# One transformer layer on one core: sixteen modulation products moved to the input projection, the retention's norm by a square root on ScalarE, and elementwise work reassigned between output and up projection

## Chip, cores and metric

One core of one Trainium2 chip runs the whole layer. The metric is device time in microseconds. The kernel before has a median of 2920.0 us over 3 runs (2919.52 to 2924.84).

## What is computed

A layer for one sequence of T = 1024 tokens with D = 1024 channels, all in fp32: a norm and a shift and scale from a condition vector, one input projection into nine parts, two mixers (retention over decayed states, and differential attention), a gated merge, and a feed-forward block with a depthwise convolution. Cut to what matters here:

```python
cond = silu(c)
mod = cond @ w_mod + b_mod
sh1, sc1, g1, sh2, sc2, g2 = split(mod, 6)
p = (x * (1 + sc1) + sh1) @ w_in
qr, kr, vr, gr, qd, kd, vd, gate_r, gate_d = project_heads(p)
y = retention(qr, kr, vr) + reversed_retention(qr, kr, vr)
y = (y - mean(y)) * rsqrt(var(y) + 1e-5)
y_ret = (silu(gr) * y) @ w_ret_out
y_dif = readout(diff_attention(qd, kd, vd)) @ w_diff_out
y_mix = (sigmoid(gate_r) * y_ret + sigmoid(gate_d) * y_dif) @ w_o
x = layer_norm(alpha * x + g1 * y_mix)
u, gate = split((x * (1 + sc2) + sh2) @ w_up)
y_ff = (gelu(dwconv(u)) * gate) @ w_down
x = layer_norm(alpha * x + g2 * y_ff)
```

## The kernel before

Every product is made in three parts. `split` (lines 83 to 86) writes the high half of an operand by a cast on ACT (line 85) and the low half by a subtraction on DVE, or on POOL where it is told so (line 71); `mm3` (line 257) then issues three matmuls, high by high, high by low and low by high. Weights come through a ring of buffers: `w_cols` and `load_split` issue the load on SP, then split it on ACT and DVE.

The stages follow one another on TensorE. After the norm of x come the projections of the attention's queries and keys, of its values (`proj_N`, tiles `pxn`), of the retention's queries and keys, and of its values (`proj_N` again). A call of `proj_N` is one group of 512 columns: four 512 KB loads of `w_in` ahead of it, and five steps of 256 tokens (four and the context). Then comes the attention, then the retention.

In the **retention** (4 heads, 4 chunks of 256 tokens, two directions) `turn` transposes keys, `update` makes a state S by matmuls (`pS`) and a DVE step and splits it (`sh` on ACT; `sl`, one half of it on DVE and one on POOL), `scores` makes the masked scores (`pa`, `am`), `outputs` makes y (`py`), copies it to `z` on ACT, takes mean and variance on DVE, and normalises; `send` transposes z, multiplies by the gate `g` and stores it. The norm's 1/sqrt is `ln_rstd`: thirteen DVE instructions on [128, 2] values (an integer estimate and three Newton steps) and one more for the shift `nb`; the normalisation is a POOL tensor_scalar on `z`.

In the **output projection** (tiles `py`, 12 groups in three passes: attention, and two halves of the retention's output) each group's product is multiplied on DVE by a sigmoid gate (`ga`) and added on POOL. Between the groups of passes two and three, two steps of the generator `mods` are taken. A step (`mod_one`, line 293) makes 256 columns of the modulation: two 512 KB loads of `w_mod` (`mr`, two buffers), one DVE tensor_scalar (line 297) and seven DVE multiply-adds (`md`, line 77), and a small matmul that sums over partitions; 8 of the 16 end in a column table (`pc`, `mcol`), the 8 of g1 and g2 in rows broadcast to all partitions (`pb`, `bmr`, `mrow1`, `mrow2`):

```python
        fill = mods()
...
                if n:
                    next(fill, None)
                    next(fill, None)
```

Then comes w_o (tiles `pxo`, eight blocks of 128 tokens). After a block `norm1` normalises it, and during the next `turned` transposes it (`pth`), scales and shifts it (`m`; half the operations on ACT, half on DVE) and splits it. The up projection forms seven products per tile of columns from sums and differences of quarters of the weights and of the tokens; `weights_first` makes the first of the former during block 7, `sum_split` the splits of the latter (`s6l`, `s7l`, `s3l`) after it, while block 7 itself is normalised and turned. Then the up projection runs 22 tiles, and the down projection with the last norm ends the kernel.

The program is written in this order, and a scheduler then sets the order of the instructions of each engine, in the retention above all; each engine and SP's queue then keep that order.

Of the kernel before, what the change touches and what calls it, by code (L numbers as in the profile page):

```python
# [8 lines left out]
F32 = mybir.dt.float32  # L9
# [55 lines left out]
def build(nc, tc, A, out, upto=99, dbg=None):  # L65
# [44 lines left out]
    d_tab = dram("d_tab", [HR, P, 896])  # L110

# [69 lines left out]

    def ln_rstd(pool, var, n, name):
        w = pool.tile([P, n], F32, name=name + "_w", tag=name + "_w")
        ts(w, var, EPS, 1.0, ALU.add, ALU.mult)
        return rsqrt(w, n, pool, name + "_rs")
# [107 lines left out]
    def mod_one(pool, raw, seg, row):  # L293
# [144 lines left out]
    with ExitStack() as ph:  # L438
# [72 lines left out]

        def proj_N(c0, dst, d0, want_ctx, func):

            ws = w_cols(w_in, c0, 512)
            for b in range(0, 10 if want_ctx else 8, 2):
# [8 lines left out]
                ST.dma_start(out=dst[b * P:b * P + 256, d0:d0 + 512].rearrange("(a p) n -> p a n", p=P), in_=st)  # L524

# [293 lines left out]
    with ExitStack() as ph:  # L819
# [34 lines left out]
        def update(h, c, d):  # L854
# [7 lines left out]
            for a in range(2):  # L862
# [8 lines left out]
                split(sh[:, a, :], sl[:, a, :], new[:, a, :], G if a else V)  # L871
# [34 lines left out]
        def outputs(h, c):  # L906
# [134 lines left out]
    with ExitStack() as ph:  # L1041
        wp = ph.enter_context(tc.tile_pool(name="p4", bufs=1))
        def mods():
            for c in range(16, 48, 2):
                o = {2: (mrow1, c - 16), 5: (mrow2, c - 40)}.get(c // 8)
                row = None if o is None else o[0][:, o[1] * P:o[1] * P + 256]
                mod_one(wp, lambda i: wp.tile([P, 1024], F32, name="mr", tag="mr", bufs=2), c, row)
                yield

# [11 lines left out]
        fill = mods()  # L1061
# [8 lines left out]
        for at, (n, g) in enumerate(groups):  # L1070
# [46 lines left out]
        for _ in fill:  # L1117
            pass
# [169 lines left out]
    for b in range(8):  # L1288
# [230 lines left out]
```

## Time and profile before

| | |
|---|---|
| median of 3 runs | 2920.0 us |
| profiled execution | 2915.08 us, its span 2913.3 us |
| busy: PE, DVE, ACT, POOL | 2798.5, 1714.0, 1058.0, 770.5 us |
| mean granted clock of TensorE | 0.984 of full speed |
| retention, 1478 to 1800 us | PE busy 291.44 us of 322 |
| output projection, 1800 to 2100 us | PE busy 276.56 us of 300 |
| w_o, 2100 to 2202 us | PE busy 101.53 us of 102 |
| passage to the up projection, 2202 to 2262 us | PE busy 37.95 us of 60 |

The stages are read by windows, since their limits differ: PE's share is 96% over all, but it leaves 30.6, 23.4 and 22.1 us idle in three of these windows. Busy time of PE includes the time in which it ran at a lower clock, so a window's mean clock belongs beside it.

### The profile page before, as it was taken

How to read it: one execution, taken by the hardware profiler on the slowest of the kernel's cores; microseconds unless marked ns; L12 is line 12 of the kernel's file. 1: busy time of each engine (PE TensorE's matmuls, PEld its weight loads, DVE VectorE, ACT ScalarE, POOL GpSimd, SP SyncE). 2: the span in 40 equal slices, each digit the busy share in tenths (PEclk: the TensorE clock that was granted, in tenths of full speed). 3: DMA queues.
4: the chain of work that ended last, by engine and by line, in shares of the span. 5: the costliest groups of instructions: out<-in, count | busy, mean ns of one | idle time of the engine just before them, and what ended most of it. 6: DMA issues, size and time to landing. Idle time of an engine off the chain costs nothing.

```text
span 2913.3 us, 34764 instructions
## 1 busy us (share of the span) xinstructions
PE 2798.5 (96%) x13610; PEld 2334.0 (80%) x13610; DVE 1714.0 (59%) x2442; ACT 1058.0 (36%) x1465; POOL 770.5 (26%) x503
## 2 busy tenths in 40 slices
PE   7999999999999999999988998999896999999997
PEld 5888888888888888888876777877685888887886
DVE  4852133201267777667779997367866555547666
ACT  4321210111245555444554554223334444444221
POOL 3321022100000000000045553034433333336744
PEclk9999999999999999999999999999998999999999
DMA  8544322422233233323143425475421322224321
GB/s 249 180 149 143 103 87 94 152 80 73 75 101 107 83 103 104 103 98 89 53 139 112 129 95 202 137 253 192 162 80 44 109 87 80 87 75 171 138 94 58
DMA packets 262309, 340.17 MB, mean 117 GB/s; under 512 B 15559, under 2 KB 193152, under 8 KB 262144
## 3 DMA queue, kind: packets, MB, share of 16 engines
q1 hardware_dynamic: 223840, 258.50, 27.8%
q10 hardware_dynamic: 38304, 79.45, 7.7%
q8 instruction: 107, 1.75, 0.2%
q14 instruction: 58, 0.48, 0.1%
HBM read 242.72 MB, written 95.16 MB: 116 GB/s over the span
## 4 chain that ended last, share of the span: by engine, by line
PE 77%; DVE 12%; DMA 5%; issue 2%; POOL 2%; ACT 1%; SPq 0%; DVEq 0%; POOLq 0%; ACTq 0%
PE pg L257 18%; PE px L257 12%; PE pxn L257 11%; PE pu L257 8%; PE pyd L257 6%; PE sp L707 5%; PE py L257 4%; PE po L257 4%; PE tp L731 2%; PE pxo L257 2%; DMA mr<-in_w_mod 2%; PE pcx L257 2%; DVE md L77 1%; DVE ql L71 1%; DVE S L77 1%
## 5 line engine op out<-in xcount | busy, mean ns | idle before, releaser
L71 DVE TENSOR_TENSOR wl<-wraw,wh 128x1024 fp32r<-128x1024 f32 (+1 forms) x234 | 311.5, 1339 | 488.8 <-ACT wh L85 485.9
L85 ACT CAST wh<-wraw 128x1024 fp32r<-128x1024 f32 (+1 forms) x234 | 219.5, 947 | 494.3 <-PE pu L257 135.7
L710 DVE TENSOR_SCALAR_CACHE_REDUCE e<-sp 128x1280 f32<-128x1280 f32 x128 | 190.6, 1489 | 106.6 <-PE sp L707 105.8
L71 POOL TENSOR_TENSOR rd<-ident,wh 128x512 fp32r<-128x512 f32 x16 | 17.7, 1107 | 852.0 <-ACT wh L85 817.1
L82 ACT ACTIVATE e<-e,m 128x1280 f32<-128x1280 f32 x128 | 175.0, 1367 | 186.0 <-DVE e L710 186.0
L71 POOL TENSOR_TENSOR wraw<-wraw 128x512 f32<-128x512 f32 x86 | 152.4, 1772 | 264.2 <-DVE wl L71 259.7
L257 PE MATMUL pg<-xH,wl 128*128 128x512 f32 x496 | 194.7, 393 | 0.0
L257 PE MATMUL pg<-xH,wh 128*128 128x512 f32 x496 | 194.7, 393 | 0.0
L257 PE MATMUL pg<-xL,wh 128*128 128x512 f32 x496 | 194.4, 392 | 0.0
L71 POOL TENSOR_TENSOR rp<-rp,rp 128x1024 f32<-128x1024 f32 x32 | 88.8, 2799 | 374.3 <-DVE rp L71 374.3
L707 PE MATMUL sp<-ks,qd 128*128 128x512 f32 (+1 forms) x768 | 174.1, 362 | 1.1 <-DVE e L710 1.1
L257 PE MATMUL py<-opH,wh 128*128 128x512 f32 x384 | 153.7, 406 | 20.1 <-DVE ga L71 15.5
L257 PE MATMUL px<-xL,wh 128*128 128x512 f32 x512 | 158.1, 390 | 0.0
L257 PE MATMUL px<-xH,wl 128*128 128x512 f32 x512 | 157.6, 389 | 0.0
L257 PE MATMUL px<-xH,wh 128*128 128x512 f32 x512 | 156.9, 391 | 0.0
L257 PE MATMUL py<-opL,wh 128*128 128x512 f32 x384 | 153.7, 400 | 1.4 <-DVE opL L71 1.3
L257 PE MATMUL py<-opH,wl 128*128 128x512 f32 x384 | 153.2, 399 | 0.0
L257 PE MATMUL pxn<-wh,xH 128*128 128x512 f32 x384 | 149.4, 389 | 0.0
L257 PE MATMUL pxn<-wl,xH 128*128 128x512 f32 x384 | 149.4, 389 | 0.0
L257 PE MATMUL pxn<-wh,xL 128*128 128x512 f32 x384 | 149.4, 389 | 0.0
L707 PEld LDWEIGHTS sp<-ks,qd 128*128 128x128 f32 x768 | 129.6, 188 | 23.4 <-DVE e L710 2.7
L257 PEld LDWEIGHTS px<-xL,wh 128*128 128x128 f32 x512 | 95.8, 188 | 21.2 <-issue 0.8
(362 smaller groups left out, 7105.6 us busy)
## 6 DMA issues: line engine op xcount, KB each, us to landing
wraw<-in_w_in SPq DMA_DIRECT2D x88, 512.0 KB, 4.0
wraw<-in_w_up SPq DMA_DIRECT2D x44, 512.0 KB, 3.7
qd<-d_qd SPq DMA_DIRECT2D x128, 128.0 KB, 3.0
mr<-in_w_mod SPq DMA_DIRECT2D x32, 512.0 KB, 5.0
ga<-d_ga SPq DMA_DIRECT2D x24, 512.0 KB, 5.4
d_u<-u SPq DMA_DIRECT2D x22, 512.0 KB, 2.6
fl<-d_u SPq DMA_DIRECT2D x22, 512.0 KB, 5.1
wraw<-in_w_down SPq DMA_DIRECT2D x22, 512.0 KB, 5.8
```

Source lines behind the costliest of these rows:

```text
L71: eng.tensor_tensor(out=o, in0=a, in1=b, op=op)
L77: V.scalar_tensor_tensor(out=o, in0=a, scalar=s, in1=b, op0=op0, op1=op1)
L82: return S.activation(out=o, in_=a, func=func, bias=bias, scale=scale, accum_out=accum)
L85: S.copy(out=h, in_=x)
L257: PE.matmul(ps[:, c:e], w, m[:, c:e], start=start and i == 0, stop=stop and i == 2, skip_group_check=more)
L707: st["pe"] = PE.matmul(sp[:, a:b], w, r["k"][c][:, a:b], start=part == 0, stop=part == 1).ins
L710: V.tensor_scalar(out=e, in0=sp[:, :TK], scalar1=-0.125, scalar2=None, op0=ALU.mult, op1=ALU.min, accum_out=m)
L731: PE.transpose(tp[:, k, :], a[:, k * P:(k + 1) * P], ident)
```

## The change

- `mods` is taken in the input projection, one step at b = 0, 4 and 8 of each `proj_N`. The rows of g1 and g2 are computed on one partition, stored by ACT's DMA queue into a new DRAM array `d_row`, and loaded broadcast into `mrow1` and `mrow2` in group 3 of the output projection.
- The retention's norm uses `rstd_shift` (lines 168 to 180): a square root on ACT, a reciprocal on DVE, seven [128, 1 or 2] instructions on POOL. `z` is normalised by two ACT activations. Both halves of `sl` go to POOL.
- `turned` scales and shifts on ACT alone. `weights_first` becomes `first_raws` (loads and POOL differences, in block 4) and `first_splits` (block 7). The large parts of `s7l` and `s3l` go from POOL to DVE.
- In the up projection product 3 comes before product 4 from the second tile on, and the copy and the addition of products 5 and 7 change places.

```diff
@@ retention
-                split(sh[:, a, :], sl[:, a, :], new[:, a, :], G if a else V)
+                split(sh[:, a, :], sl[:, a, :], new[:, a, :], G)
...
-            rs = ln_rstd(misc, mv[:, :, 1], 2, "lnr")
-            nb = misc.tile([P, 2], F32, name="nb", tag="nb")
-            stt(nb, mv[:, :, 0], -1.0, rs, ALU.mult, ALU.mult)
+            rstd_shift(misc, mv[:, :, 0], mv[:, :, 1], 2, "lnr")
             for b in range(2):
-                ts(zs[b], zs[b], rs[:, b:b + 1], nb[:, b:b + 1], ALU.mult, ALU.add, G)
+                act(zs[b], zs[b], AF.Identity, bias=mv[:, b, 0:1], scale=mv[:, b, 1:2])
@@ mod_one
-            bmr = pool.tile([P, 256], F32, name="bmr", tag="bmr")
-            SP.dma_start(out=bmr, in_=A["b_mod"][:, seg * P:seg * P + 256].broadcast_to([P, 256]))
-            pb = small_ps("pb")[:, 0:256]
-            PE.matmul(pb, onesr.bitcast(F32), md, start=True, stop=True)
-            tt(row, pb, bmr, ALU.add)
+            bmr = pool.tile([1, 256], F32, name="bmr", tag="bmr")
+            SP.dma_start(out=bmr, in_=A["b_mod"][:, seg * P:seg * P + 256])
+            pb = small_ps("pb")[0:1, 0:256]
+            PE.matmul(pb, ones, md, start=True, stop=True)
+            tt(bmr, pb, bmr, ALU.add)
+            ST.dma_start(out=row, in_=bmr)
@@ proj_N
+                if b % 4 == 0:
+                    next(fill, None)
@@ output projection
-                if n:
-                    next(fill, None)
-                    next(fill, None)
+                    for t, r in ((mrow1, 0), (mrow2, 1)):
+                        SP.dma_start(out=t, in_=d_row[r:r + 1, :].broadcast_to([P, D]))
@@ turned
-                if q:
-                    ts(y[:, k, cut], pt[:, j, :], hs[:, 0, k:k + 1], hs[:, 1, k:k + 1], ALU.mult, ALU.add)
-                else:
-                    act(y[:, k, cut], pt[:, j, :], AF.Identity, bias=hs[:, 1, k:k + 1], scale=hs[:, 0, k:k + 1])
+                act(y[:, k, cut], pt[:, j, :], AF.Identity, bias=hs[:, 1, k:k + 1], scale=hs[:, 0, k:k + 1])
@@ w_o
             if n == 5:
+                if b == 4:
+                    first_raws()
                 if b == 7:
-                    weights_first(misc_tile("t2", 1)[:, 0:512])
+                    first_splits()
@@ passage
-    sum_split("7", slice(0, 384), G)
-    sum_split("7", slice(384, 512))
-    sum_split("3", slice(0, 384), G)
-    sum_split("3", slice(384, 512))
+    for n, c in (("6", slice(384, 512)), ("7", slice(0, 384)), ("7", slice(384, 512)), ("3", slice(0, 512))):
+        sum_split(n, c)
@@ up projection
             product(chain, f, 7, False)
-            S.copy(out=g[:, c_hi], in_=chain)
-            tt(g[:, c_hi], g[:, c_hi], p5, ALU.add)
+            tt(g[:, c_hi], g[:, c_hi], chain, ALU.add)
...
+            product(p5, f, 3, False)
+            tt(g[:, c_lo], g[:, c_lo], p5, ALU.add)
             product(chain, f, 4, False)
             S.copy(out=raw[:, c_hi], in_=chain)
-            product(p5, f, 3, False)
-            tt(g[:, c_lo], g[:, c_lo], p5, ALU.add)
```

Three places show what moves. First, DVE in the third pass of the output projection, before (`wl` is the low half of a weight, `ga` the gating):

```order
L77 SCALAR_TENSOR_TENSOR md_16473<-mr_16471,condT_77,md_16473 128x256
L71 TENSOR_TENSOR ga_16339<-py3_16342,ga_16339 128x512
L71 TENSOR_TENSOR wl_16498<-wraw_16494,wh_16497 128x1024
L77 SCALAR_TENSOR_TENSOR md_16473<-mr_16471,condT_77,md_16473 128x256 x3
L71 TENSOR_TENSOR ga_16343<-py3_16346,ga_16343 128x512
L71 TENSOR_TENSOR mrow2_14709<-pb_16466,bmr_16464 128x256
L297 TENSOR_SCALAR md_16627<-mr_16623,condT_77 128x256
L71 TENSOR_TENSOR wraw_16671<-wraw_16671,mrow1_14713 128x1024
L77 SCALAR_TENSOR_TENSOR md_16627<-mr_16623,condT_77,md_16627 128x256 x3
L77 SCALAR_TENSOR_TENSOR md_16627<-mr_16625,condT_77,md_16627 128x256 x3
L71 TENSOR_TENSOR ga_16339<-py3_16342,ga_16339 128x512
L77 SCALAR_TENSOR_TENSOR md_16627<-mr_16625,condT_77,md_16627 128x256
```

and the same place after the change:

```order
L71 TENSOR_TENSOR wl_16266<-wraw_16263,wh_16265 128x1024
L71 TENSOR_TENSOR ga_16141<-py3_16144,ga_16141 128x512
L71 TENSOR_TENSOR ga_16275<-py3_16278,ga_16275 128x512
L71 TENSOR_TENSOR wl_16272<-wraw_16269,wh_16271 128x1024
L71 TENSOR_TENSOR ga_16279<-py3_16282,ga_16279 128x512
L71 TENSOR_TENSOR wraw_16535<-wraw_16535,mrow1_14858 128x1024
L71 TENSOR_TENSOR ga_16275<-py3_16278,ga_16275 128x512
L71 TENSOR_TENSOR wl_16527<-wraw_16523,wh_16526 128x1024
L71 TENSOR_TENSOR ga_16279<-py3_16282,ga_16279 128x512
L71 TENSOR_TENSOR wl_16539<-wraw_16535,wh_16538 128x1024
```

The `md` chains that stood between one gating and the next are gone from this queue.

Second, SP's queue at the passage from the attention's values to the retention's queries and keys, before (`wraw` is a load of weights):

```order
L219 DMA wraw_2401<-in_w_in 128x2x512
L447 DMA sin_2675<-in_k_rope_ret 128x1024
L447 DMA cos_2673<-in_k_rope_ret 128x1024
L219 DMA wraw_2407<-in_w_in 128x2x512
L219 DMA wraw_2677<-in_w_in 128x4x256
L219 DMA wraw_2683<-in_w_in 128x4x256
L219 DMA wraw_2799<-in_w_in 128x4x256
L219 DMA wraw_2805<-in_w_in 128x4x256
```

and after:

```order
L215 DMA wraw_2465<-in_w_in 128x2x512
L215 DMA wraw_2788<-in_w_in 128x4x256
L303 DMA bmr_2318<-in_b_mod 1x256
L263 DMA mr_2523<-in_w_mod 128x4x256
L263 DMA mr_2525<-in_w_mod 128x4x256
L303 DMA bmr_2441<-in_b_mod 1x256
L263 DMA mr_2646<-in_w_mod 128x4x256
L263 DMA mr_2648<-in_w_mod 128x4x256
L215 DMA wraw_2794<-in_w_in 128x4x256
L215 DMA wraw_2910<-in_w_in 128x4x256
L215 DMA wraw_2916<-in_w_in 128x4x256
```

Loads of `w_mod` and `b_mod` now stand between the loads of `w_in`.

Third, ACT in the retention, before (`g` is the Silu of the gate):

```order
L85 CAST qh_12534<-qs_12532 128x512
L922 COPY z_12319<-py_12320 128x512
L81 ACTIVATE g_12220<-g_12220 128x1024
L943 DMA d_zT_68<-g_12005 128x4x256
L85 CAST sh_12236<-S1_12108 128x512
L85 CAST qh_12540<-qs_12538 128x512
L85 CAST sh_12236<-S1_12108 128x512
L81 ACTIVATE kdh_12271<-pt_12266,ktab_85 128x256
L81 ACTIVATE kdh_12312<-pt_12307,ktab_85 128x256
L922 COPY z_12319<-py_12343 128x512
```

and after:

```order
L85 CAST sh_12334<-S0_11695 128x512
L81 ACT_TABLE_LOAD
L81 ACTIVATE lnr_rs_12263<-mv_12215,eps_89 128x2
L81 ACTIVATE kdh_12209<-pt_12198,ktab_86 128x256
L85 CAST sh_12334<-S0_11695 128x512
L81 ACTIVATE kdh_12209<-pt_12198,ktab_86 128x256
L81 ACT_TABLE_LOAD
L81 ACTIVATE g_12276<-g_12276 128x1024
L85 CAST kh_12775<-kraw_12561 128x512
L85 CAST qh_12732<-qs_12730 128x512
L85 CAST ah_12330<-am_12315 128x512
L81 ACTIVATE z_12216<-z_12216,mv_12215 128x512 x2
```

A load of a function table now stands ahead of each square root `lnr_rs` and of nearly each Silu of `g`: the program has 34 such loads, where it had 8. The normalisation of `z` is new on ACT.

## Rows read from the trace of the kernel before

**Rows 1.** Busy time by window: start:end, us, each engine's busy us, clock, DMA share, GB/s.
```profile
57.00:245.00 188.00, 188.00 (x930) 159.66 (x930) 123.00 (x159) 54.32 (x97) 48.67 (x27) 1.00 0.54 166
...
1478.00:1800.00 322.00, 291.44 (x1426) 236.54 (x1424) 296.25 (x626) 165.29 (x285) 172.24 (x118) 0.97 0.38 123
1800.00:2100.00 300.00, 276.56 (x1178) 225.15 (x1179) 186.56 (x276) 89.53 (x107) 95.31 (x63) 0.95 0.60 202
...
2202.00:2262.00 60.00, 37.95 (x136) 28.95 (x135) 39.44 (x48) 25.80 (x37) 17.61 (x9) 0.80 0.16 53
2262.00:2650.00 388.00, 387.12 (x1689) 316.80 (x1689) 207.40 (x205) 166.60 (x205) 150.57 (x83) 1.00 0.27 87
```

**Rows 2.** PE's waits, 1478 to 1800 us: us in total, times, longest.
```profile
PE pS L257 <- DVE S L77: 6.2, 5, 2.9
...
PE pS L257 <- DVE kdl L77: 2.7, 3, 1.9
...
PE pS L257 <- DVE nb L77: 0.5, 1, 0.5
```

**Rows 3.** DVE groups, 1478 to 1800 us: count | busy us, mean ns | idle before, releasers.
```profile
L71 DVE TENSOR_TENSOR sl<-S,sh 128x512 fp32r<-128x512 f32 x32 | 33.3, 1040 | 0.5 <-ACT sh L85 0.3
...
L137 DVE TENSOR_SCALAR lnr_rs<-lnr_w 128x2 int32<-128x2 int32 x15 | 12.3, 822 | 0.5
...
L77 DVE SCALAR_TENSOR_TENSOR nb<-mv,lnr_rs 128x2 f32<-128x2 f32 x15 | 4.9, 326 | 0.3
```

**Rows 4.** POOL groups, over the whole span.
```profile
L71 POOL TENSOR_TENSOR sl<-S,sh 128x512 fp32r<-128x512 f32 x32 | 47.3, 1478 | 53.2 <-ACT sh L85 48.1 <-DVE kl L71 4.9
L74 POOL TENSOR_SCALAR z<-z,lnr_rs,nb 128x512 f32<-128x512 f32 x32 | 31.3, 988 | 29.6 <-DVE nb L77 23.0 <-DMA qraw<-d_qr 6.4
L71 POOL TENSOR_TENSOR ln_e<-ln_e,ln_rs 128x2 f32<-128x2 f32 x8 | 1.6, 195 | 1.5 <-DVE ln_rs L173 1.3
```

**Rows 5.** ACT groups: casts of the retention's queries, and the last norm's activations.
```profile
L85 ACT CAST qh<-qs 128x512 fp32r<-128x512 f32 x32 | 19.8, 618 | 10.2 <-POOL qs L71 6.7 <-DVE oT L77 2.4 <-PE pS L257 1.0
L81 ACT ACTIVATE acc<-acc,mv 128x512 f32<-128x512 f32 x14 | 10.7, 809 | 15.4 <-POOL mv L71 15.4
```

**Rows 6.** ACT's timeline, 1561 to 1566 us: start, us, instruction.
```profile
1562.02 1.28 ACT L81 ACT_TABLE_LOAD   x1 [0.35 <-DMA g<-d_gT]
1563.31 1.06 ACT L81 ACTIVATE g<-g 128x1024 f32<-128x1024 f32 x1
```

**Rows 7.** PE's waits, 1800 to 2100 us.
```profile
PE py L257 <- DVE ga L71: 15.5, 5, 5.5
```

**Rows 8.** DVE group, 1800 to 2100 us.
```profile
L77 DVE SCALAR_TENSOR_TENSOR md<-mr,condT,md 128x256 f32<-128x256 f32 x112 | 70.9, 634 | 6.2 <-DMA mr<-in_w_mod 3.8
```

**Rows 9.** Busy time by window, as rows 1, after one of these waits.
```profile
1957.50:1964.30 6.80, 5.50 (x13) 4.34 (x14) 5.57 (x10) 1.15 (x1) 2.30 (x2) 0.50 0.94 290
```

**Rows 10.** PE's waits, 2100 to 2262 us.
```profile
PE pth L1162 <- ACT x L81: 12.3, 3, 10.4
```

**Rows 11.** DVE's timeline, 2212 to 2226 us.
```profile
2213.45 3.90 DVE L71 TENSOR_TENSOR opL<-m,opH 128x512 fp32r<-128x512 f32 x1
...
2219.87 1.75 DVE L71 TENSOR_TENSOR s6l<-m,s6h 128x1536 fp32r<-128x1536 f32 x1
2221.53 3.37 DVE L71 TENSOR_TENSOR ln_rs<-ln_rs,ln_e 128x1 f32<-128x1 f32 x1
```

**Rows 12.** POOL's timeline, the same stretch.
```profile
2212.86 3.93 POOL L71 TENSOR_TENSOR s7l<-m,s7h 128x1536 fp32r<-128x1536 f32 x1
...
2221.38 3.51 POOL L71 TENSOR_TENSOR s3l<-m,s3h 128x1536 fp32r<-128x1536 f32 x1 [1.63 <-ACT s3h L85]
```

**Rows 13.** Costliest groups and DMA issues of the page: splits and loads of weights.
```profile
L71 DVE TENSOR_TENSOR wl<-wraw,wh 128x1024 fp32r<-128x1024 f32 (+1 forms) x234 | 311.5, 1339 | 488.8 <-ACT wh L85 485.9
L85 ACT CAST wh<-wraw 128x1024 fp32r<-128x1024 f32 (+1 forms) x234 | 219.5, 947 | 494.3 <-PE pu L257 135.7
...
wraw<-in_w_in SPq DMA_DIRECT2D x88, 512.0 KB, 4.0
```

More of the change, by code (lines that the diff above doesn't have):

```diff
@@ L110, in build @@
     d_tab = dram("d_tab", [HR, P, 896])
+    d_row = dram("d_row", [2, D])
     def const(name, shape, dt=F32):
@@ L180, in rstd_shift @@
         tt(mean, mean, var, ALU.mult, G)
[L182 to L185, printed above, removed]
     smp = top.enter_context(tc.tile_pool(name="small", bufs=1, space=PSUM))
@@ L510, in proj_ret, with mods @@
                     ST.dma_start(out=dst[g, half, :, T:], in_=cs)
+        def mods():
+            for c in range(16, 48, 2):
+                row = {2: (0, c - 16), 5: (1, c - 40)}.get(c // 8)
+                if row is not None:
+                    row = d_row[row[0]:row[0] + 1, row[1] * P:row[1] * P + 256]
+                mod_one(wp, lambda i: wp.tile([P, 1024], F32, name="mr", tag="mr", bufs=2), c, row)
+                yield
+        fill = mods()
         def proj_N(c0, dst, d0, want_ctx, func):
@@ L1039, in residual @@
         tt(t, t, bc[:, 1, :], ALU.add, V if b < 4 else G)
[L1041 to L1048, printed above, removed]
+    if True:
         def operand(src, n, k):
@@ L1116, in build @@
                     residual(1)
-        for _ in fill:
-            pass
         with tc.issue_after(ga_load):
@@ L1225, in weights_3, with first_raws, first_splits @@
         half_split(w["t14"], w["u"])
-    def weights_first(t2):
+    def first_raws():
         u, g = up_raws(0)
-        b1 = ring_pair()
-        half_split(b1, u)
-        tt(u[:, c_lo], g[:, c_lo], u[:, c_lo], ALU.subtract, G)
-        tt(t2, g[:, c_hi], u[:, c_lo], ALU.subtract, G)
+        t14 = res.tile([P, 1024], F32, name="t14")
+        t2 = res.tile([P, 512], F32, name="t2")
+        tt(t14[:, c_lo], g[:, c_lo], u[:, c_lo], ALU.subtract, G)
         tt(g[:, c_lo], g[:, c_hi], g[:, c_lo], ALU.subtract, G)
-        tt(u[:, c_hi], u[:, c_hi], t2, ALU.subtract, G)
-        W[0] = {"b1": b1}
+        tt(t2, g[:, c_hi], t14[:, c_lo], ALU.subtract, G)
+        tt(t14[:, c_hi], u[:, c_hi], t2, ALU.subtract, G)
         u1 = ring["pool"].tile([P, 1024], F32, name="wraw", tag="wraw", bufs=ring["raws"])
         SP.dma_start(out=u1.rearrange("p (a b) -> p a b", b=P), in_=w_up[:, :, P:2 * P])
-        b1 = ring_pair()
-        half_split(b1, u1)
-        W[0]["t14"] = ring_pair()
-        half_split(W[0]["t14"], u)
+        W[0], W[1] = {"raws": (u, g, t14, t2)}, {"u": u1}
+    def first_splits():
+        u, g, t14, t2 = W[0]["raws"]
+        for f, name, src in ((0, "b1", u), (1, "b1", W[1]["u"]), (0, "t14", t14)):
+            W[f][name] = ring_pair()
+            half_split(W[f][name], src)
         W[0]["t32"] = ring_pair()
@@ L1245, in weights_first @@
         half_split(W[0]["t32"], t2, 512, 512)
-        g1 = ring["pool"].tile([P, 1024], F32, name="wraw", tag="wraw", bufs=ring["raws"])
-        SP.dma_start(out=g1.rearrange("p (a b) -> p a b", b=P), in_=w_up[:, :, FF + P:FF + 2 * P])
-        tt(u1[:, c_lo], g1[:, c_lo], u1[:, c_lo], ALU.subtract, G)
-        tt(g1[:, c_lo], g1[:, c_hi], g1[:, c_lo], ALU.subtract, G)
-        W[1] = {"u": u1, "g": g1, "b1": b1}
+        W[1]["g"] = ring["pool"].tile([P, 1024], F32, name="wraw", tag="wraw", bufs=ring["raws"])
+        SP.dma_start(out=W[1]["g"].rearrange("p (a b) -> p a b", b=P), in_=w_up[:, :, FF + P:FF + 2 * P])
         W[0]["b22"] = ring_pair()
@@ L1368, in build @@
             chain, p2, p5, raw, g = F[f]
-            if f == 0:
-                product(p5, f, 5, True)
-                product(chain, f, 6, False)
-                S.copy(out=g[:, c_lo], in_=chain)
-            else:
-                product(chain, f, 6, False)
-                S.copy(out=g[:, c_lo], in_=chain)
-                product(p5, f, 5, True)
+            turn56 = (5, 6) if f == 0 else (6, 5)
+            for n in turn56:
+                if n == 6:
+                    product(chain, f, 6, False)
+                    S.copy(out=g[:, c_lo], in_=chain)
+                else:
+                    product(p5, f, 5, True)
+                    S.copy(out=g[:, c_hi], in_=p5)
             product(chain, f, 7, False)
-            S.copy(out=g[:, c_hi], in_=chain)
-            tt(g[:, c_hi], g[:, c_hi], p5, ALU.add)
+            tt(g[:, c_hi], g[:, c_hi], chain, ALU.add)
             if 0 < f < NF - 1:
```

5 lines of the change are left out of this document (3 added, 2 removed).

## The prediction

> **What bounds the kernel now.** I read the busy time by window first, because a share over the whole span hides where the time goes. In the queries' projection and the up projection PE has no idle time worth naming; in the retention, the output projection and the passage to the up projection PE is idle for 30.6, 23.4 and 22.1 us, and its mean clock there is 0.97, 0.95 and 0.80 of full speed [rows 1]. The change can only gain in these three; elsewhere it can only cost. PE's waits say who is late in each. In the retention, twelve rows of waits on DVE add up to 22.2 us, from 6.2 on the state S to 0.5 on nb [rows 2], and DVE is the busiest engine there, 296.25 us of 322 against PE's 291.44 [rows 1]. In the output projection the gating `ga` is late five times, 15.5 us in all [rows 7]; it shares DVE's queue with the `md` chains [rows 8]. In the passage PE waits for block 7 of x, 10.4 us of the 12.3 at once [rows 10].
>
> The clock makes a wait cost twice. Just behind one of the output's waits the granted clock is 0.50, the level of 1.2 GHz in place of 2.4, for 6.8 us [rows 9]: half of that, 3.4 us, is lost beside the wait itself. Over a window, a mean clock of 0.97 is a loss of at most 0.03 x 322 = 9.7 us, and 0.95 one of 15 [rows 1].
>
> **Retention: -26 us.** DVE loses the norm's eight groups, from 12.3 us down to 4.9, together 70.4 for 15 of the 16 norms, and its half of `sl`, 33.3 us [rows 3]. It gains sixteen small reciprocals, which at the 0.33 us of nb [rows 3] are 5 us at most. So 296 falls to about 198, and PE, at 291 with its slow stretches, becomes the longest. ACT gains 32 activations of 128 x 512; a cast of this size takes 618 ns, one with two per-partition operands 809 [rows 5]: 20 to 26 us, and I take 20, since the cast is from the same stage. It gains sixteen square roots, about 5 us at nb's price [rows 3], and 26 table loads of 1.28 us [rows 6], 33 us. ACT goes from 165 to about 223 of 322. POOL gains 47.3 us of `sl`, loses 31.3 of `z`, and gains sixteen times seven tiny steps of 0.195 us [rows 4], 22 us: 172 becomes 210. No engine but PE stays above 230.
>
> Of the 22.2 us of waits I leave the three on `kdl`, 5.8 us in all, the largest row 2.7 [rows 2], because that chain goes through ACT, which gets fuller. 16.4 us go, and with them most of the slow stretches, 9.7 us: -26. The bounds: all of PE's idle time and clock loss goes, 30.6 + 9.7 = -40; or a third of the waits and one stretch go, about -8. What is late next is `sh` and the table loads ahead of it.
>
> The trace shows the activation that needed a table starting 10 ns after the load ended (1562.02 + 1.28 against 1563.31) [rows 6], so 1.28 us is the price taken. The Trainium skill, "ScalarE: Activation LUTs", section What ACT_TABLE_LOAD costs, adds a drain and puts each switch at 2.66 us; by that the 26 switches would be 69 us in place of 33, ACT would stand near 259 and, with seven round trips on the path as in the first rival below, the retention would be 11 us slower rather than 8 faster. What the drain would lie in front of, the row doesn't show; I stay with it.
>
> **Output projection: -26 us.** The sixteen `mods` leave: 112 multiply-adds, 70.9 us [rows 8], of DVE's 186.56 [rows 1]. The `ga` step is then behind weight splits only, as the DVE excerpts of the order show. The 15.5 us of waits [rows 7] go, and three slow stretches that follow them, one shown [rows 9], 3 x 3.4 = 10.2. The rest of the 15 us of clock loss lies at the start of the stage, where its first operands are being loaded, and stays. Sixteen pairs of 512 KB loads leave too, in the stage with the highest DMA share, 0.60 [rows 1]. Bounds: -30 (other small waits go too) and -15 (the waits go, the slow stretches stay). Loading two rows back in group 3 is needed only by the w_o weights in groups 9 and later; nothing.
>
> **Passage: -11 us.** Block 7's chain meets POOL twice. A split on DVE takes 3.90 us beside POOL's 3.93 of `s7l`, and an operation on one column takes 3.37 beside POOL's 3.51 of `s3l`; both pairs end together, and a DVE split of three times the first one's width takes 1.75 [rows 11, 12]. With both on DVE these delays, about 7.3 us, leave the chain, and one slow stretch the length of the one shown, 3.4 us [rows 9], with them. The new DVE work, two splits of 1.75 or a little over, may stand in the chain: -4. Differences of the first weights made in block 4 may save more: -16. Here the trace speaks for the Trainium skill, "SBUF — State Buffer", section Who interferes with whom, which calls the port that DVE and GpSimd share an exclusive lock; by it the `sl` that moves to POOL could hold up DVE in the retention for up to the 47 us that move, which would fit into the 124 us that DVE then has free.
>
> **Input projection: +2 us.** PE is busy throughout here [rows 1], so the `mods` can only cost. Its small matmuls merely change stage. DVE takes them in with 65 of 188 us free in its fullest window [rows 1]; if a third of them still delayed a PE step, by the 1.6 us that the output's 26 us make per `mod`, it is +8; if none, 0. `turned` moves 32 operations to ACT, each smaller than the 0.62 us cast, over eight blocks: nothing, under cover of w_o's matmuls. In the up projection PE is busy 387.12 of 388 us [rows 1], so a new order of the products and of copies has nothing to gain, and its copies the same cover as now: 0.
>
> **Sum.** -26 - 26 - 11 + 2 = -61. The profiled execution took 2915.08 us, so the changed one should take 2854; the median of the runs is 4.9 above it, and 2920 - 61 = **2859**. All low ends together give -86, all high ends -19; taken as independent they give about 20 either way, 2839 to 2880.
>
> **Rivals.**
> ACT takes DVE's place in the retention. Each norm's root and each gate's Silu now changes the table; thirteen round trips of 2 x 1.28 us [rows 6] stand in ACT's queue ahead of `sh` and `kdh`. If seven lie on the path, that is 18 us: the retention gains 8, total -43, 2877. For it: ACT is in order, and PE already waits on it. Against it: 100 us free on ACT. That functions should be batched by table is also the Trainium skill's rule ("ScalarE: Activation LUTs", section Table sets: the hidden batching unit); no run here shows it so far. Chance 0.18.
>
> The retention runs to PE's bound: -40 in place of -26, total -75, 2845. For it: every other engine is under 230. Against: the state's chain from DVE to ACT to POOL is a chain of latencies, which more room does not shorten. Chance 0.10.
>
> The waits of the output projection are for operands and not for `md`: DVE's excerpt keeps the weight splits between the gatings, and loads run at a share of 0.60. Then a third of the 26 us is gained, total about -44, 2876. Against: the `md` group alone is 38% of DVE's busy time. Chance 0.05.
>
> **Slower:** SP's queue in the input projection. Loads of `w_mod` use two buffers, so one waits on SP until an `md` chain of two steps before has read its buffer, and the loads of `w_in` stand behind it in the same queue, as the excerpt shows. This decides once such a wait outlasts the lead that the ring of weight buffers gives; then each of six groups of `proj_N` starts without its weights, for 4.0 us of a load and four times 0.95 + 1.34 of splits [rows 13], 13 us: 79 us, total +18, **2938**. Against: DVE is free there, so a chain ends soon after its data land, and the scheduler places the loads ahead. Chance 0.04.
>
> The cases that cancel (the ACT rival in full, and half of this one): no change, chance 0.03. The forecast itself has 0.60.
>
> **How the numbers follow.** 0.2%, 5.8 us, is about what a measurement tells from no change. Forecast, ACT, PE's bound and operands are faster: 0.93; same 0.03; slower 0.04. The range of the forecast is widened at the top for the ACT rival with its own spread, and below for PE's bound: 2832 to 2892.
>
> **What would show it.** Right: DVE near 200 us in the retention and PE's waits on S gone; no wait on `ga` of several us; `s7l` and `s3l` on DVE, no column operation of 3 us; the queries' and values' projections as long as before. Wrong: waits of PE on `sh`, `sl` or z of more than 15 us in the retention (ACT or POOL in DVE's place), waits on `wh` in `proj_N` (SP's queue), or an output projection still near 300 us.

## The result

The changed kernel has a median of 2888.2 us (2883.4 to 2894.5, 4 runs) against 2922.4 of the kernel before (4 runs): a ratio of 0.988, 95% interval 0.9864 to 0.9896, so 34 us faster. The forecast was 61 us faster, 2859, within 2832 to 2892. The sign held, and so, in the main, did the mechanisms named for the gains; a little over half of the size came.

The profiled execution of the changed kernel took 2888.07 us, with a span of 2886.3 against 2913.3. Windows of the changed kernel, cut at the same stages as in [rows 1] (input from 57 us, the second values' projection, retention, output projection, passage, up projection):

```profile
57.00:246.50 189.50, 187.83 (x928) 159.20 (x927) 128.95 (x175) 53.89 (x96) 52.27 (x27) 1.00 0.60 180
...
556.50:781.50 225.00, 225.00 (x1001) 184.03 (x1000) 50.78 (x91) 33.44 (x33) 4.59 (x2) 1.00 0.38 127
...
1492.00:1808.00 316.00, 290.98 (x1431) 237.75 (x1430) 217.32 (x370) 220.23 (x354) 211.17 (x223) 0.97 0.40 129
1808.00:2090.00 282.00, 271.43 (x1164) 222.21 (x1165) 113.33 (x120) 96.71 (x120) 100.12 (x70) 0.97 0.46 153
...
2186.00:2246.00 60.00, 49.52 (x208) 38.89 (x207) 39.02 (x48) 31.94 (x48) 14.00 (x10) 0.91 0.23 70
2246.00:2622.00 376.00, 375.04 (x1626) 306.41 (x1627) 215.59 (x198) 158.39 (x198) 137.95 (x78) 1.00 0.27 86
```

The work moved as forecast: in the retention DVE went from 296 to 217 us, ACT from 165 to 220 (223 was forecast), POOL from 172 to 211 (210). Yet the stage hardly shrank, and its mean clock is 0.97 as before. To see where the time went, each trace is cut at the first matmul that PE starts in a stage (the retention from its first `pS` to the first `py` of the output projection, 1481.4 to 1798.6 us before and 1497.7 to 1808.0 after). The lengths in us, from one profiled execution each; "passage" goes from the last matmul into `pxo` to the 200th behind the first into `pu`, and the last row is what is left of the span:

| stage | before | after | difference | forecast |
|---|---|---|---|---|
| input projections | 732.5 | 744.9 | +12.4 | +2 |
| attention and gates | 713.2 | 717.6 | +4.4 | 0 |
| retention | 317.2 | 310.3 | -6.9 | -26 |
| output projection | 302.1 | 275.7 | -26.4 | -26 |
| w_o | 98.8 | 101.9 | +3.1 | 0 |
| passage | 111.8 | 99.6 | -12.2 | -11 |
| up and down projection | 602.0 | 601.0 | -1.0 | 0 |

Two of three gains came as forecast in size; the retention's did not, and the input projection cost six times what it should. w_o varies between 98 and 102 us over all fourteen traces of this study, with the same edits too, so its difference lies within what a single execution leaves open. The attention takes 712.0 to 713.2 us in the three kernels that lack most of the edits (before, e1_mods, e2_ret) and 713.9 to 718.4 in the eleven others; a lengthening of some 3 us may be real, and its cause is not shown.

PE's waits in the changed kernel, the retention's first, from 1492 to 1808 us:

```profile
PE pz L948 <- ACT z L81: 4.3, 4, 1.7
PE py L253 <- ACT opH L85: 4.0, 1, 4.0
PE pS L253 <- DVE S L77: 3.6, 4, 1.5
PE pa L253 <- DVE am L71: 2.8, 2, 2.4
PE pa L253 <- DVE ql L71: 2.6, 2, 1.7
PE pq L766 <- DVE kdl L77: 2.0, 1, 2.0
...
PE py L253 <- POOL sl L71: 1.2, 4, 0.5
```

Against [rows 2], waits on DVE fell from 22.2 us in all to 13.9; those on ACT rose from 5.1 to 9.3, and two of them head the list. In the output projection, 1808 to 2090 us, the gating is late for 6.0 us in place of 15.5 [rows 7]:

```profile
PE py L253 <- DVE ga L71: 6.0, 3, 3.0
PE py L253 <- ACT opH L85: 4.0, 1, 4.0
PE pz L948 <- ACT z L81: 3.6, 1, 3.6
```

The wait for `opH` is the one of the list before; it ends at the cut, at 1807.97 us. The last wait is that of the retention's last z. ACT's groups of the retention answer to [rows 5]:

```profile
L81 ACT ACT_TABLE_LOAD x26 | 33.4, 1283 | 15.3 <-DMA g<-d_gT 8.2 <-DVE mv L155 5.1 <-DVE g L71 1.6
...
L81 ACT ACTIVATE z<-z,mv 128x512 f32<-128x512 f32 x30 | 22.8, 807 | 13.4 <-POOL mv L71 13.4
...
L81 ACT ACTIVATE lnr_rs<-mv,eps 128x2 f32<-128x2 f32 x15 | 4.4, 296 | 5.0 <-DVE mv L155 4.8
```

26 table loads take 33.4 us. ACT also stands idle in front of them, 8.2 us for the gate's data: the Silu is in its queue, and what is behind it waits.

### The profile page after: what moved, and what is told of

It is laid out like the page before. It is cut to its first block, busy times and chain, and to the rows that moved or that the text cites. A ratio compares the mean times of both kernels' runs of the same rounds, so it can differ in the third digit from the quotient of the medians.

```text
span 2886.3 us, 34740 instructions
## 1 busy us (share of the span) xinstructions
PE 2793.8 (97%) x13610; PEld 2327.8 (81%) x13610; DVE 1626.6 (56%) x2139; ACT 1122.6 (39%) x1570; POOL 809.8 (28%) x613
## 4 chain that ended last, share of the span: by engine, by line
PE 81%; DMA 5%; DVE 5%; POOL 3%; ACT 3%; issue 3%; SPq 0%; ACTq 0%; DVEq 0%; POOLq 0%
PE pg L253 18%; PE pxn L253 11%; PE px L253 11%; PE pu L253 8%; PE py L253 8%; PE pyd L253 6%; PE sp L717 5%; PE po L253 4%; PE pxo L253 2%; PE tp L741 2%; PE pcx L253 2%; DMA g<-d_gT 1%; DVE acc L71 1%; PE pS L253 1%; DMA wraw<-in_w_in 1%
## 5 line engine op out<-in xcount | busy, mean ns | idle before, releaser
L71 DVE TENSOR_TENSOR wl<-wraw,wh 128x1024 fp32r<-128x1024 f32 (+1 forms) x233 | 319.8, 1386 | 248.1 <-ACT wh L85 241.5
L81 ACT ACTIVATE st<-pxn 128x1024 f32<-128x1024 f32 x30 | 30.8, 1027 | 235.0 <-PE pxn L253 231.0
```

Source lines behind the costliest of these rows:

```text
L71: eng.tensor_tensor(out=o, in0=a, in1=b, op=op)
L81: return S.activation(out=o, in_=a, func=func, bias=bias, scale=scale)
```

## Experiments

Each ran beside the kernel before and has a profile. The stage lengths of all of them, from one profiled execution each, are in one table below. The six kernels with the changed retention as it stands (after, e2, e3, e8, e9, e10) have retentions of 310.3 to 312.9 us, so a difference of 3 us there tells nothing.

**The parts alone.** e1_mods is the kernel before with the modulation alone moved (the edits in `mod_one`, `mods`, `proj_N` and the output projection):

```diff
+                if b % 4 == 0:
+                    next(fill, None)
...
-                if n:
-                    next(fill, None)
-                    next(fill, None)
```

> The kernel before with the modulation products alone moved to the input projection (rows through DRAM). Theory M (the moved small matmuls cost PE time where PE has none free): input stages about 9 us longer (16 products at 0.4 to 0.6 us), output projection about 26 shorter, retention and passage unchanged; total 15 to 19 us below the kernel before. Rival N (the 10 us that the input stages gained have another cause, and the move costs 2 as predicted): total 24 us below. Rival O (the output's gain comes from the other edits): total within 5 us of before.

Measured: 2909.6 us, ratio 0.9957 (0.9943 to 0.997) to before. Input +11.7, output -21.9, every other stage within 2: the price of the input stages belongs to the move. That is theory M in kind; the whole is 14 us below before, a little less than its 15 to 19.

e2_ret is the kernel before with the retention's edits alone:

```diff
-            rs = ln_rstd(misc, mv[:, :, 1], 2, "lnr")
...
+            rstd_shift(misc, mv[:, :, 0], mv[:, :, 1], 2, "lnr")
...
+                act(zs[b], zs[b], AF.Identity, bias=mv[:, b, 0:1], scale=mv[:, b, 1:2])
```

> The kernel before with the retention's edits alone (root on ACT, normalisation on ACT, both low halves on POOL). Theory: the edit moves 80 us off DVE but PE's waits there are mostly short latencies of one step behind another and the start of the stage, so the retention gains 5 to 10 us, not 26; total 4 to 12 us below before. Rival (the retention by itself gains 26, and the small gain of the full change is an interplay with the other edits): total 20 to 30 below.

Measured: 2913.8 us, ratio 0.9967 (0.9954 to 0.998); the retention is 5.7 us shorter. Its small gain is its own and no interplay.

e3_nopass is the changed kernel without the edits between w_o and the up projection:

```diff
-                act(y[:, k, cut], pt[:, j, :], AF.Identity, bias=hs[:, 1, k:k + 1], scale=hs[:, 0, k:k + 1])
+                if q:
+                    ts(y[:, k, cut], pt[:, j, :], hs[:, 0, k:k + 1], hs[:, 1, k:k + 1], ALU.mult, ALU.add)
...
-                if b == 4:
-                    first_raws()
...
+    sum_split("7", slice(0, 384), G)
```

> The changed kernel with the edits between w_o and the up projection undone (scale and shift half on DVE, first weights all in block 7, large parts of s7l and s3l on POOL). Theory: the passage is 10 to 13 us longer again, 120 in place of 100 with small shifts of the stages ahead; total 9 to 14 us above the changed kernel. Rival (the passage is shorter only because DVE reaches it without a backlog from the modulation): within 4 us of the changed kernel.

Measured: 2900.6 us, ratio 0.9923 (0.9911 to 0.9936); the passage is 113.6 us, 14.0 more than in the changed kernel. So the parts are worth 14, 10 and 12 us by medians, together 36 against 34: they add up to the whole.

**What holds the retention.** e4_notable leaves the root out (a pass-through activation of the same size stands in its place), and the table loads vanish with it:

```diff
-        act(t, var, AF.Sqrt, bias=eps[:, 0:1])
+        act(t, var, root, bias=eps[:, 0:1])
...
+            rstd_shift(misc, mv[:, :, 0], mv[:, :, 1], 2, "lnr", root=AF.Identity)
```

> The changed kernel with the square root of the retention's norm replaced by a pass-through activation on ACT, so that the root is left out of the computation, and 26 table loads, 33 us of ACT, with it. Theory T (the table loads stand in front of the state's casts and of z and took DVE's place): retention 10 to 18 us shorter than in the changed kernel. Theory L (the remaining waits are latencies and the start and end of the stage): retention within 4 us of the changed kernel's 310.

Measured: 2869.0 us, ratio 0.9815 (0.9802 to 0.9829); the retention takes 294.9 us, 15.4 less. Theory T: the table loads cost close to half of their 33 us on the path, though ACT is busy for only 220 us of 316. The Silu stays in this kernel, and ACT still stands idle in front of it for the gate's data, 13.7 us in the retention; so that wait by itself is not what costs.

e6_tanh removes the alternation without leaving out anything, since the tanh is computed beside the attention's exponentials, from the table that is loaded there:

```diff
                     S.copy(out=sg, in_=pg)
+                    if i < 16:
+                        th = wp.tile([P, 512], F32, name="th", tag="th", bufs=1)
+                        act(th, sg, AF.Tanh, scale=0.5)
+                        stt(sg, th, 1.0, sg, ALU.add, ALU.mult)
...
-            with tc.issue_after(R["turned"]):
-                act(g, g, AF.Silu)
...
-                tt(g[:, :, cut], pz, g[:, :, cut], ALU.mult)
+                stt(g[:, :, cut], pz, 0.5, g[:, :, cut], ALU.mult, ALU.mult)
```

> The changed kernel with the retention's gate computed where the gates are projected: silu(x) = x (1 + tanh(x/2)) / 2, the tanh on ACT beside the attention's exponentials and one more DVE step there, the factor 0.5 in the product with z. ACT then has no Silu in the retention and the 26 extra table loads go: theory T gives a retention 15 us or more shorter than in the changed kernel, near 292, as with the root left out, and the attention unchanged to 5 us longer (32 more steps of 0.7 us each on ACT and DVE, which have over 200 us free there): total 2866 to 2874. Rival (the attention's chains of exponentials are delayed by what is added): attention 10 us or more longer, total 2880 or above.

Measured: 2870.4 us, ratio 0.9814 (0.9801 to 0.9828) to before; its interval lies below that of the changed kernel. It is the fastest complete kernel here; the retention's 14.8 us less are just short of the 15 expected. ACT's table loads in the retention, 1492 to 1795 us, are down to one, and the two groups that were added to the attention (781 to 1480 us) hide:

```profile
L81 ACT ACT_TABLE_LOAD x1 | 1.3, 1283 | 0.0
```

```profile
L77 DVE SCALAR_TENSOR_TENSOR sg<-th,sg 128x512 f32<-128x512 f32 x32 | 22.1, 692 | 4.1 <-ACT th L81 3.6
L81 ACT ACTIVATE th<-sg 128x512 f32<-128x512 f32 x32 | 20.2, 631 | 0.6
```

The attention is 718.4 us against 717.6, the retention 295.5 against 310.3.

e7_newton puts the norm's 1/sqrt back on DVE, in the changed kernel (fifteen small instructions a norm, and `nb`):

```diff
-            rstd_shift(misc, mv[:, :, 0], mv[:, :, 1], 2, "lnr")
+            rs = ln_rstd(misc, mv[:, :, 1], 2, "lnr")
+            nb = misc.tile([P, 2], F32, name="nb", tag="nb")
+            stt(nb, mv[:, :, 0], -1.0, rs, ALU.mult, ALU.mult)
...
-                act(zs[b], zs[b], AF.Identity, bias=mv[:, b, 0:1], scale=mv[:, b, 1:2])
+                act(zs[b], zs[b], AF.Identity, bias=nb[:, b:b + 1], scale=rs[:, b:b + 1])
```

> The changed kernel with the norm's 1/sqrt back on DVE by the integer estimate and Newton steps (z still normalised on ACT, low halves on POOL): no table loads beyond 8, ACT 38 us less, DVE 70 more, about 287 of 310. Theory T (the loads cost 15 us, which is more than DVE's relief by the root was worth): retention 298 to 304, total 6 to 12 below the changed kernel. Rival D (DVE near its limit brings back the waits of before): retention 310 or longer, total at or above the changed kernel.

Measured: 2909.1 us, ratio 0.9944 (0.9932 to 0.9956). The retention is 328.3 us, 18 longer, where I had expected it 6 to 12 shorter: rival D. Its window, and its longest waits of PE there:

```profile
1492.00:1825.00 333.00, 295.69 (x1425) 238.68 (x1425) 286.53 (x593) 181.94 (x310) 185.37 (x118) 0.96 0.38 119
```

```profile
PE pt L859 <- DVE g L71: 7.7, 6, 3.4
PE pa L258 <- DVE am L71: 4.6, 3, 2.7
PE pS L258 <- DVE kdl L77: 4.3, 3, 1.9
PE pS L258 <- DVE S L77: 4.0, 6, 1.5
PE pa L258 <- DVE ql L71: 3.7, 2, 2.6
```

DVE is back at 286.5 us, and all five are on DVE. So the root's leaving DVE is worth 33 us in this setting (328.3 against 294.9 in e4_notable, which has the Silu too, and 295.5 in e6_tanh), and the table loads give 15 of them back.

e5_sl puts one half of the state's low part back on DVE, in the changed kernel; e12_sl does so in the tanh kernel; e11_root moreover normalises z on POOL again:

```diff
-                split(sh[:, a, :], sl[:, a, :], new[:, a, :], G)
+                split(sh[:, a, :], sl[:, a, :], new[:, a, :], G if a else V)
...
-                act(zs[b], zs[b], AF.Identity, bias=mv[:, b, 0:1], scale=mv[:, b, 1:2])
+                ts(zs[b], zs[b], mv[:, b, 1:2], mv[:, b, 0:1], ALU.mult, ALU.add, G)
```

> The changed kernel with one half of the state's low part back on DVE: POOL loses 47 us of its 211 in the retention, DVE gains 33 on its 217. Theory T (ACT's table loads hold the retention): neither matters, within 4 us of the changed kernel. Rival P (POOL's queue holds it, sl and the root's small steps behind one another): retention 5 us or more shorter. Rival D (DVE's relief is what gained): retention 3 to 6 us longer.

> The kernel with the tanh gate and one half of the low parts back on DVE, z still on ACT. POOL falls from 214 to about 167 us, DVE rises from 222 to 255. Theory R: within 4 us of the tanh kernel. Rival P (POOL's queue of sl and small steps holds the end of z's chain): 5 us or more below.

> The kernel with the tanh gate (the changed kernel without the 26 table loads) and, of the retention's edits, the root alone: z normalised on POOL and one half of the low parts on DVE again. Theory R (the gain in the retention comes from the root leaving DVE, and the other two moves cost as much as they give, as the 328 us with the Newton steps back on DVE suggest against 317 before): retention 288 to 296, total at or below the tanh kernel's 2870. Rival (z on ACT and the low part on POOL are worth their part): retention 5 us or more longer than its 295.

Measured: 2881.7 us, ratio 0.9853 (0.9838 to 0.9869), for e5_sl: 6 us below the changed kernel, with intervals that overlap and a retention of 310.0 against 310.3. The execution with the profile is the slowest of its four, 2887.7, so where the others gained is not shown. 2876.1, ratio 0.984 (0.9819 to 0.986), for e12_sl, and 2876.2, ratio 0.9838 (0.9817 to 0.9859), for e11_root: both slightly above the tanh kernel, intervals overlapping, their retentions 295.4 and 297.8 against 295.5. In the retention neither the move of sl nor that of z is worth more than 2 us once the root has left DVE: theory R. Its totals missed: it had the whole within 4 us of the tanh kernel for e12_sl and at or below it for e11_root, and both are 6 us above. In the traces their output projections are 283.9 and 280.7 us against 276.8. The two moves may even cost where DVE is full, since the retention of e7_newton, with both of them and the root on DVE, is 11 us longer than that of the kernel before. Why, in either case, is not settled.

**What shortens the passage.** Three single edits are undone in the changed kernel: e8_s73 has the large parts of `s7l` and `s3l` on POOL, e9_turned half of the scale and shift on DVE, e10_first the first weights all in block 7.

```diff
-    for n, c in (("6", slice(384, 512)), ("7", slice(0, 384)), ("7", slice(384, 512)), ("3", slice(0, 512))):
-        sum_split(n, c)
+    sum_split("6", slice(384, 512))
+    sum_split("7", slice(0, 384), G)
+    sum_split("7", slice(384, 512))
+    sum_split("3", slice(0, 384), G)
+    sum_split("3", slice(384, 512))
```

```diff
-                act(y[:, k, cut], pt[:, j, :], AF.Identity, bias=hs[:, 1, k:k + 1], scale=hs[:, 0, k:k + 1])
+                if q:
+                    ts(y[:, k, cut], pt[:, j, :], hs[:, 0, k:k + 1], hs[:, 1, k:k + 1], ALU.mult, ALU.add)
+                else:
+                    act(y[:, k, cut], pt[:, j, :], AF.Identity, bias=hs[:, 1, k:k + 1], scale=hs[:, 0, k:k + 1])
```

```diff
-                if b == 4:
-                    first_raws()
                 if b == 7:
-                    first_splits()
+                    weights_first(misc_tile("t2", 1)[:, 0:512])
```

> The changed kernel with the large parts of s7l and s3l back on POOL, all else as changed. Theory C (DVE steps that run beside them are stretched to their length, two such meetings on block 7's chain): passage 6 to 9 us longer than the changed kernel's 99.6, with DVE steps of over 3 us beside POOL's. Rival W (it is the first weights made early, and the scale and shift on ACT, that shorten the passage): within 3 us.

> The changed kernel with half of the scale and shift of the transposed x back on DVE. The large parts of s7l and s3l alone brought back 3.5 of the passage's 12 us and all three edits together 14 (113.6 against 99.6). Theory A (ACT's scale and shift takes work off DVE, which holds the end of block 7's chain): passage 4 to 7 us longer. Theory F (the first weights made early are what gives the rest): within 2 us.

> The changed kernel with the first weights' loads, differences and splits all in block 7, as before the change. Theory F: passage 6 to 10 us longer, with POOL's differences and DVE's splits beside block 7's chain. Theory A: within 3 us.

Measured: 2889.8 us, ratio 0.9879 (0.9865 to 0.9893); 2888.4, ratio 0.9884 (0.9865 to 0.9902); 2887.8, ratio 0.988 (0.9861 to 0.99). None can be told from the changed kernel by its time. Their passages are 103.1, 100.8 and 104.2 us against 99.6: +3.5, +1.2 and +4.6, 9.3 in sum where all three together are +14.0. The seven kernels that have all three edits take 98.1 to 99.6, so +1.2 is hardly clear of their spread; and since w_o ends where the passage begins, the two should be read together too: 201.9, 203.0 and 204.6 us, against 196.3 to 201.5 in those seven and 212.3 in e3_nopass. PE's wait for x in the passage is 12.8 us with all three undone, but 3.4, 2.9 and 3.4 with one. So what each edit is worth by itself is not resolved; that the three together are worth 10 us or more is. Theories C and F and their rivals are too simple: C had 6 to 9 us, A 4 to 7, F 6 to 10. The meetings of DVE and POOL do come back with e8_s73. DVE's timeline there, 2188 to 2230 us, then POOL's:

```profile
2194.25 3.46 DVE L77 SCALAR_TENSOR_TENSOR nb<-mv,ln_rs 128x1 f32<-128x1 f32 x1
...
2204.83 3.51 DVE L71 TENSOR_TENSOR wl<-wraw,wh 128x512 fp32r<-128x512 f32 x1
```

```profile
2194.20 3.49 POOL L71 TENSOR_TENSOR s7l<-m,s7h 128x1536 fp32r<-128x1536 f32 x1 [1.66 <-ACT s7h L85]
...
2204.35 3.44 POOL L71 TENSOR_TENSOR s3l<-m,s3h 128x1536 fp32r<-128x1536 f32 x1 [3.09 <-ACT s3h L85]
```

Two DVE instructions take as long as the POOL instruction beside them, but only the first, `nb`, stands on block 7's chain.

The stage lengths of all, in us, cut as above (input, attention, retention, output, w_o, passage):

```
before      732.5  713.2  317.2  302.1   98.8  111.8
after       744.9  717.6  310.3  275.7  101.9   99.6
e1_mods     744.2  712.5  319.0  280.2   98.7  111.7
e2_ret      735.8  712.0  311.5  304.4   99.5  110.9
e3_nopass   745.7  714.5  311.4  277.4   98.7  113.6
e4_notable  742.4  714.7  294.9  275.8  102.0   99.3
e5_sl       746.5  713.9  310.0  278.3   99.9   98.6
e6_tanh     743.8  718.4  295.5  276.8  101.5   99.3
e7_newton   746.1  715.7  328.3  282.9   98.1   98.2
e8_s73      744.3  716.1  312.9  277.7   98.8  103.1
e9_turned   744.5  716.2  311.0  276.4  102.2  100.8
e10_first   745.2  714.3  311.8  276.1  100.4  104.2
e11_root    742.7  716.7  297.8  280.7   99.2   98.7
e12_sl      744.5  717.5  295.4  283.9  100.1   98.1
```

## Why the prediction was right, and where its size was off

By its own sum the time should have been 2839 to 2880 us. 2888 lies above that, and within 2832 to 2892 only because the top had been widened for the ACT rival; that the range held is owed to the rival, not to the forecast's terms.

**Retention: -7 in place of -26, the largest error, and the first rival came true.** That rival had the gain at 8 us, by seven round trips of 2.57 us on the path; the loads cost 15 (e4_notable, e6_tanh), and the retention gained 7. The step that failed is "No engine but PE stays above 230", taken to mean that ACT's added 58 us are covered. The busy times were right to 3 us on ACT and 1 on POOL, and 19 too low on DVE, still far from full. Most of these 19 are a matter of counting: records that follow one another closely overlap, so that DVE's records add up to 332 us before and 238 after, 94 less where 99 was forecast, while the busy time falls by 79. A share of 70% says nothing of where in the queue the new work stands. ACT's timeline in the changed kernel shows it:

```profile
1596.27 1.28 ACT L81 ACT_TABLE_LOAD   x1 [0.96 <-DMA g<-d_gT]
1597.56 1.06 ACT L81 ACTIVATE g<-g 128x1024 f32<-128x1024 f32 x1
1598.53 0.56 ACT L932 COPY z<-py 128x512 f32<-128x512 f32 x1
1598.99 0.62 ACT L85 CAST qh<-qs 128x512 fp32r<-128x512 f32 x1
1599.51 1.52 ACT L81 ACTIVATE z<-z,mv 128x512 f32<-128x512 f32 x2
```

and PE's timeline who waits:

```profile
1600.38 0.66 PE L948 MATMUL pz<-ident,z 128*128 128x128 f32 x4 [1.66 <-ACT z L81]
```

The wait for the gate's data, the load and the Silu take 0.96 + 1.28 + 1.06 us of a queue in which z stands behind them, and PE loses 1.66. The end of the stage shows it again. The last load waits for the gate's data; the load, the Silu and a copy follow, and only then come the first operands of the output projection, for which PE waits 4.0 us, the second row of its list above:

```profile
1804.58 1.28 ACT L81 ACT_TABLE_LOAD   x1 [1.34 <-DMA g<-d_gT]
1805.87 1.06 ACT L81 ACTIVATE g<-g 128x1024 f32<-128x1024 f32 x1
...
1807.30 3.22 ACT L85 CAST opH<-mvraw 128x512 fp32r<-128x512 f32 x6
```

From the last `py` of the retention to the first of the output projection it is 6.8 us, against 2.1 before, 2.8 in e4_notable and 1.6 in e6_tanh (6.7 to 8.4 in the six kernels with the changed retention): 4 to 5 of the loads' 15 us lie here. The sign that was given for this rival, more than 15 us of waits on `sh`, `sl` or z, did not show: they are 5.9 us, and the wait on `opH` was not on its list.

The second part of that term was the clock, 9.7 us: the window's mean is 0.97 still. The low clock lies at the start of the stage, 1498 to 1548 us in the changed kernel, ahead of its first root at 1557, where PE waits on S, am, ql and kdl one step behind the other; from there on it is 1.00:

```profile
1498.00:1548.00 50.00, 39.41 (x175) 31.29 (x174) 42.39 (x63) 27.73 (x49) 41.24 (x25) 0.86 0.42 133
1548.00:1798.00 250.00, 240.64 (x1204) 197.07 (x1203) 168.78 (x297) 183.86 (x292) 166.19 (x191) 1.00 0.37 117
```

I had read the stage as one, and so credited the norm with waits of a start in which it has no part: there PE's waits on DVE are 9.9 us, where they were 9.1 before (1481.5 to 1552 us); behind the start they fell from 13.1 to 4.0. Without the loads the retention is 22 us shorter than before, near the 26 forecast: the mechanism, DVE's relief, was right, and e7_newton shows it by itself.

On the drain the trace decides. Between the end of an instruction and the load behind it there are 0.02 us, and 0.01 behind the load, where nothing else was waited for (ACT's timeline, 1570 to 1576 us):

```profile
1569.65 0.61 ACT L85 CAST kh<-kraw 128x512 fp32r<-128x512 f32 x1
1570.16 0.62 ACT L85 CAST sh<-S 128x512 fp32r<-128x512 f32 x1
1570.80 1.28 ACT L81 ACT_TABLE_LOAD   x1
1572.10 0.30 ACT L81 ACTIVATE lnr_rs<-mv,eps 128x2 f32<-128x2 f32 x1
```

The 1.38 us that the Trainium skill, "ScalarE: Activation LUTs", section What ACT_TABLE_LOAD costs, puts beside each load are not there; ACT's 220 us agree with 1.28 a load. What a load puts off is a little more than that: the casts `kh` and `sh` overlap by 0.10 us, and beside a load nothing does, so `lnr_rs` starts about 1.4 us later than it would right behind `sh` (an estimate from these rows). The rule of the same page, section Table sets: the hidden batching unit, spoke against the change, and e6_tanh agrees with it: with the two functions kept apart the stage is 14.8 us shorter.

**Input projection: +12 in place of +2.** The term failed at "its small matmuls merely change stage": in a stage without free time that alone is +9. PE's timeline around one of them:

```profile
257.25 0.39 PE L253 MATMUL pxn<-wh,xL 128*128 128x512 f32 x1
257.56 0.59 PE L305 MATMUL pb<-md,ones 128*1 128x256 f32 x2
258.09 0.50 PE L253 MATMUL pxn<-wh,xH 128*128 128x512 f32 x1
258.42 0.39 PE L253 MATMUL pxn<-wl,xH 128*128 128x512 f32 x1
258.65 0.39 PE L253 MATMUL pxn<-wh,xL 128*128 128x512 f32 x1
```

From one `pxn` to the next it is 0.84 us in place of 0.23, and to the one behind that 0.33: 0.71 for a `pb`. Around the four small matmuls of a `pc` it is 0.60 and 0.31 (611.86, 612.46, 612.77 us): 0.45. Eight of each make 9.3 us, the 9.5 by which the two values' projections are longer (108.6 to 112.1 and 217.4 to 223.4). Nor was this work free where it came from. In the kernel before, four of the sixteen stood beside a wait of PE (1.2 to 5.5 us) in the output projection; the other twelve stood in a full run of `py`, like this one:

```profile
1924.61 0.39 PE L257 MATMUL py<-opH,wl 128*128 128x512 f32 x1
1924.84 0.59 PE L309 MATMUL pb<-md,onesr 128*128 128x256 f32 x2
1925.08 0.58 PE L257 MATMUL py<-opH,wh 128*128 128x512 f32 x1
1925.50 0.39 PE L257 MATMUL py<-opL,wh 128*128 128x512 f32 x1
```

By the same count this `pb` cost 0.43 us, and a `pc` there 0.46: 5 to 6 us for the twelve. So most of the price did change stage, as the prediction said, but it had counted it in neither; what is new is the `pb` with a single row of output (`128*1`), 0.28 us dearer, and the four that had stood beside waits. The wait that the slower rival feared, for weights behind SP's queue, isn't there: PE names no wait for weights in the input projections, and the chance of 0.04 looks right. The sign that the projections would be as long as before did not hold.

**Output projection: -26.4, forecast -26.** Waits on `ga` went from 15.5 to 6.0 us, 9.5 of the 15.5 forecast. The stage's mean clock went from 0.95 to 0.97, a loss of 15 us down to 8, where 10 was forecast to go. The twelve small matmuls that left gave 5 to 6 us that the forecast had not counted, and the waits for `opH` in the stage, 4.6 us before, are gone; the changed kernel has its own ahead of the cut, in the retention. e1_mods alone gives -21.9; in the ten other kernels that have the move the stage takes 275.8 to 283.9 us, so the agreement within 1 us is in good part chance.

**Passage: -12.2, forecast -11; the size was right, the cause too narrow.** I put it all on two meetings with POOL. In the changed kernel the operation on one column that took 3.37 us [rows 11] takes 0.16, and `s7l` on DVE 1.76:

```profile
2194.34 0.16 DVE L71 TENSOR_TENSOR ln_rs<-ln_rs,ln_e 128x1 f32<-128x1 f32 x1
2194.45 1.76 DVE L71 TENSOR_TENSOR s7l<-m,s7h 128x1536 fp32r<-128x1536 f32 x1
```

The wait for x, 12.3 us [rows 10], is down to (2084 to 2262 us)

```profile
PE pth L1158 <- ACT x L81: 1.0, 2, 0.6
```

But with `s7l` and `s3l` back on POOL only 3.5 of 14.0 us return, and that wait is 3.4 us; the early first weights hold 4.6, and the rest comes only with all three. It looks as if several small things free the chain of block 7 and stand in for one another; that reading is argued from these lengths. That DVE's instruction lasts as long as the POOL instruction beside it, four times in the rows shown here (one of them, `opL`, ends 0.56 us behind it and not with it, as the prediction had read), agrees with the Trainium skill, "SBUF — State Buffer", section Who interferes with whom, on the shared port.

**Up and down projection:** 601.0 against 602.0 us, as forecast nothing; the new order was not run by itself.

The sum by the forecast's own steps: retention +19 and input +10 against it, and the attention's and w_o's +7, of which most other kernels with the same edits show less; -61 became -27 between the two profiled executions, and -34 between the medians.

## What to carry to other kernels

Where work moves to an engine that is busy for 70% of a stage, ask what stands behind it in that engine's queue, and not whether there is room: a function table that alternates puts its loads ahead of everything that follows. Keep functions of different tables in different stages (here a tanh beside exponentials, in place of a Silu beside roots, took 18 us off the whole kernel). Small matmuls cost their whole interval wherever PE is full, so they have to be counted both in the stage that they leave and in the one that they enter. The start and the end of a stage should be costed apart from its steady part.

## What the runs showed of the hardware

A load of a function table took ACT 1.283 us, 26 times out of 26 in the retention, with gaps of 0.01 to 0.02 us to its neighbours where nothing else was waited for; by the overlap that it breaks, a switch puts off what follows by about 1.4 us. A DVE instruction on one value per partition took 3.4 us beside a POOL instruction of 3.5, where it takes 0.16 alone; which DVE instruction is hit moved from kernel to kernel, from `ln_rs` to `nb` and `wl`. A sum over partitions of 256 columns, with a single row of output, put off PE by 0.71 us in the middle of a run of 512-column products that take 0.23 each; with 128 rows of output it was 0.43.
